# Filler matmuls, a re-sorted weight queue and a new operand order in the first stage of a hybrid SSD/Conformer layer

## The chip, the cores and the metric

The kernel runs on one core of a Trainium2 chip. The metric is the device time of one execution in microseconds (us), the median of three runs. A profiled execution gives the trace that the rows further down come from.

## What is computed

One layer of a hybrid backbone over 128 context tokens and 512 latent tokens, 1024 channels, in float32. The conditioning vector (one for the latent tokens, one for the context) is turned into six modulation vectors; the normed tokens are scaled and shifted by the first two of them and go through one input projection, which feeds an SSD mixer and a Conformer branch; an output projection and a gated ConvFFN follow. The change lies wholly in the first lines:

```python
def trunk_layer(x, cond, prm, init_f, init_b, rows):
    mod = jax.nn.silu(cond) @ prm["w_ada"] + prm["b_ada"]
    sh1, sc1, g1, sh2, sc2, g2 = [m[:, None, :] for m in jnp.split(mod, 6, axis=-1)]

    h = rms_norm(x, prm["norm_mix_pre"]) * (1 + sc1) + sh1
    proj = h @ prm["w_in"]
    z, xbc, dt_raw, cf_in = jnp.split(
        proj, [SSD_WIDTH, SSD_WIDTH + CONV_CH, SSD_WIDTH + CONV_CH + 2 * SSD_HEADS], axis=-1)
    ...
```

## The kernel before

The tokens lie with channels on the 128 partitions, as eight tiles T0 to T7 (channel block k) of 640 columns: 512 latent and 128 context tokens. "The first stage" is what runs until the first three products of the input projection are done, about the first 57 us.

**Norm.** ACT squares each token tile (L498), and TensorE adds up the squares over the channels with a column of ones (`colsum`, L473). That matmul is narrow: it writes 32 partitions, and four of them, one in each 32-column group of the array (`tile_position=(0, 32 * j)`), take a quarter of the tokens each. ACT takes the square root (L487), DVE the reciprocal (L488), and `spread` (L481) copies the result to all 128 partitions with four full-width matmuls. DVE multiplies the token tiles by it (L523).

**Condition.** `ada_first(s)` (L437 to L446) computes slice s of four: eight weight tiles of 128x512, 256 KB each, go against the condition `cts` in narrow matmuls again, four for each tile (L441). ACT copies the sum out (`adar`, L444), TensorE transposes it (L423), DVE adds the bias (`modv`, L432) and forms the factor `asc` (L529, L530). Slice s serves the channel blocks 2s and 2s+1: DVE applies it (L534) and splits the result into a high part on ACT (L400, tiles H0 to H7) and a low part on DVE (L402, H8 to H15).

**First products.** Three units of the input projection (g0, a0, B0) are accumulated in psum P0, P2 and P1. `mm3` (L415) makes every product of three full-width matmul pairs (384 and 256 columns): weight high x token low, high x high, low x high, where it is the first of a sum, and high x high first elsewhere. Unit weights arrive in `wr` (512 KB, L287), ACT takes their high part `wh` (L311) and POOL the low part `wl` (L313). `dt_product` (L507) is a narrow one again; L604 (`idhl`) is the last step of that branch.

**Queues and order.** Every transfer of the stage is issued by SP, one after the other: the condition, the eight token tiles, then the weight tiles of the four slices (slice 0 in T8 to T15, slice 1 in S4 to S11, slice 2 in M0 to M7 and HL, slice 3 in T8 to T15 again), the constants `csts`, the parameters `prms`, the weights of dt (`wdts`) and the units' `wr`. The order of the instructions on each engine is neither the program's nor a scheduler's: a table `ORDER` gives it by hand, one list of instruction numbers for each engine, and `issue_in_order` (L166) ties every instruction behind the one ahead of it in the list. In the table of before, the transfers of the slices are mixed with each other.

Of the kernel before, what the change touches and what calls it, by code (L numbers as in the profile page):

```python
# [13 lines left out]
P = 128  # L14
# [23 lines left out]
for _name, _w in (("b_ada", 48), ("g_mix_pre", 8), ("g_mix_post", 8), ("g_ffn_pre", 8),  # L38
# [12 lines left out]
0-31 36-49 32-34 50-53 35 54-90 104-105 102-103 91-101 116-119 106 120-126 107-115 127 187-191 175-180 192  # L51
181-182 193 173-174 140-172 194-196 183-186 211-242 197-198 258-259 243 128-129 246-252 260-263 130-139
199-210 270 253-257 264-265 284-289 244-245 282-283 320-327 271-281 290-291 266-269 296 292-294 308-311
297-298 295 312-319 299-307 328-332 341-374 399-402 375-378 403 379-385 404 386-388 405-434 447-450 435-445
451-464 446 465-487 495 488-492 496-506 493-494 507-522 543-550 523 551-560 524-535 561-567 536 568-574
537-542 575-590 645-648 333-335 649-684 336-339 685-690 693-719 691-692 720-725 340 389-393 726-758 789-796
759 394-398 797-799 760-768 595 591-594 800-803 769-776 804-818 777-788 819-836 878-916 596-603 608 604-607
926-931 917-923 932-946 924-925 947-970 974-983 971-973 984-1005 609-620 1006-1014 1022 621-644 1023-1028
1015-1019 1029 1020-1021 1030-1048 837-841 1070-1073 1049 1074-1087 1050-1056 1088-1094 1057-1069 1095-1117
846-849 842-845 854-857 850-853 1118-1146 1207-1213 1147 1214-1216 1148-1163 1217 1164-1165 874-877 858-873  # L60
1218-1226 1255-1256 1227-1249 1257-1275 1250-1251 1276-1283 1252-1254 1284-1290 1170 1166-1169 1291-1294
1303-1314 1295-1302 1315-1337 1351-1352 1338-1350 1353-1374 1450-1452 1375-1381 1453-1470 1382-1398
1171-1178 1183-1186 1179-1182 1471-1484 1187-1206 1485-1517 1546 1518 1547-1554 1519-1521 1399-1403
1522-1524 1555-1556 1525 1557-1567 1526-1532 1568-1577 1533-1545 1578-1609 1683-1684 1610-1623 1404-1408
1624-1626 1685-1700 1627-1641 1701-1718 1409-1432 1441-1442 1433-1435 1443-1444 1436-1440 1719-1723
1731-1743 1724-1729 1744-1745 1730 1746-1755 1449 1445-1448 1756-1811 1827-1830 1812-1814 1642-1646
1815-1823 1831-1835 1824-1826 1836-1866 1916 1867 1917-1918 1647-1682 1919 1868-1869 1920 1870-1874
1921-2010 2012-2017 2011 2018-2022 1875-1879 2023-2080 2149-2150 2081-2089 2151-2157 2090-2103 2158-2164
2104-2107 2165-2179 1884-1887 1880-1883 1892-1895 1888-1891 2197-2201 1912-1915 1896-1911 2202-2244
2180-2196 2357-2386 2112 2108-2111 2245-2272 2387-2416 2117-2120 2113-2116 2417-2446 2125-2128 2121-2124  # L70
2145-2148 2129-2144 2447-2467 2507-2518 2468 2519 2273-2276 2317-2320 2277-2280 2321-2324 2469-2476
2520-2531 2477-2491 2325-2335 2341-2344 2336-2340 2281-2290 2492-2495 2291-2300 2496-2506 2532 2301-2310
2533-2534 2311-2312 2345-2352 2535-2545 2313-2316 2546-2552 2567-2585 2553-2562 2586-2593 2563-2566 2594
2353-2356 2597-2613 2595-2596 2614-2615 2810-2829 2759-2770 2645-2648 2621-2637 2649 2638-2639 2650-2658
2640-2641 2659-2661 2642-2644 2693-2704 2616-2620 2669-2676 2705-2709 2662-2668 2717 2710-2711 2677-2682
2712 2683-2686 2718-2727 2687-2689 2728 2713 2729-2740 2714 2690-2692 2830-2831 2771-2780 2832-2835
2781-2790 2836-2841 2843 2741-2742 2715-2716 2792-2794 2743-2747 2791 2748-2755 2844-2847 2756-2758
2795-2799 2848-2849 2800-2809 2850-2860 2894-2896 2960-2963 2897-2915 2964-2966 2916-2924 2967-2973
2925-2926 2974-2987 2861-2892 2842 3092-3094 3026 2988-2990 3027-3035 2991-2992 3036-3045 3095 3046-3057
3096-3099 2893 3058 3125 3100-3102 2927-2942 2993-3014 2943-2950 3015-3024 2951-2958 3103-3107 2959  # L80
3108-3122 3126-3133 3123-3124 3134-3146 3203-3204 3147-3150 3025 3151-3158 3059-3089 3176-3183 3090
3159-3165 3205-3207 3166-3175 3184-3188 3208-3210 3189-3198 3211-3218 3199-3202 3091 3219-3236 3301-3310
3237-3245 3311 3246-3251 3312 3252-3253 3270-3276 3313-3317 3338 3318-3319 3277-3284 3320-3327 3332-3337
3339-3348 3254-3269 3285-3300 3328-3331 3349-3373 3388-3390 3397-3398 3380-3387 3374-3375 3399 3410-3412
3406-3409 3377 3376 3391-3393 3400-3402 3413-3415 3419 3422-3423 3378 3420 3379 3394-3396 3421 3403-3405
3424 3431 3416-3418 3425 3428 3426 3429 3432-3433 3430 3437-3439 3446-3448 3427 3434-3436 3471-3476 3443
3440-3442 3449-3451 3493-3504 3509-3510 3444-3445 3452 3511-3513 3539-3556 3455-3470 3477-3492 3514-3524
3505-3508 3557-3570 3525-3538 3453-3454 3572-3575 3644-3647 3668-3669 3576-3578 3648-3650 3670-3674
3579-3581 3571 3651-3653 3582-3584 3654-3656 3675-3680 3585-3587 3657-3659 3681-3682 3620-3623 3588-3590
3624-3625 3591-3593 3596-3598 3594-3595 3599-3619 3626-3643 3660-3667 3683-4059 4061-4081 4060 4082-5548  # L90
5597-5615 5549-5596 5616-5658 5693-5695 5659-5664 5696-5716 5665-5692 5717-6599 6665-6668 6600-6664
6669-6676""",
    "DVE": """
0 3-4 1-2 13-16 18-19 17 5 20 11-12 23-26 6 27-30 7-9 21-22 33-35 38-39 36 10 37 31-32 41-42 46 43-44 40 47
45 48 51 49 52 50 53-54 84-90 111-114 55-56 91-94 69 95-96 119-122 57-60 97-100 61-68 101-102 70-71 75
123-125 103-106 72 152-155 76-77 82 78 73 107-109 79-80 74 81 110 83 126-129 163 130-135 115-118 136 156
137-141 164-165 142-146 193 147-151 194-196 166-171 204 172-180 157-159 181 160 182-183 161 184 162 197
205-206 185-192 207-210 234 238-239 235-237 211 200 212 240-241 201 213-214 198-199 215-216 242-245 217-219
246 202-203 220-223 253 224-233 254-261 247 262-266 248-250 267 283-286 268 251-252 269 298 270-275 287
276-282 299-300 289 301-313 288 290-291 328-331 314 292-293 315 332 316-317 339 318 294 296 295 297 319-326  # L100
333 340-341 327 334 342-347 335 348 336 349 337-338 350-354 371-374 355-359 375 382 360-370 383-384 376
385-386 377 387-393 416-419 379 378 394-396 380 420 381 397-401 463 432 464-465 428 402-403 447 404 442
448-450 405-407 443 408-410 421-422 444 411 424 423 451 445-446 412-413 426 414-415 425 427 454 429-430 455
452-453 434 439 436 438 435 456 433 457 437 440 460 431 459 458 461-462 441 466-467 469-470 472 478 473
475-476 468 479-480 482-485 481 471 474 488 477 486 489 487 495 498 496 502 501 497 491 490 505 508 494
499-500 515 509 503-504 518 492 512 493 519 506-507 510-511 520-522 537 523 513-514 516 525 527-528 530 526
529 532-533 538 531 535 524 540 534 557 536 539 517 541-543 545 544 558 546 548 550 547 559 552 560-561
563-564 566 549 551 567 565 553 568 554-556 569 571-575 570 562 576-585 589 586-588 593 590 594 591-592 595
597 596 598 601-602 599-600 605 603-604 606-612 615-616 613-614 617-749 1053 750-1046 1049-1051 1047-1048
1052 1054-1063 1065 1064 1066-1075""",  # L110
    "Activation": """
0-3 7 6 4 8 5 9-11 15 18 12 19 17 21-22 13 20 24 23 25 35 26-27 32-33 14 30 28-29 16 48-49 47 31 56-58 61 64
50-51 62 34 67 65-66 63 52-53 37-38 79 116 80 54 36 39 55 71 68 40-43 120 44-45 72 46 117 121-122 81 69-70
59-60 73-76 82-83 123 91 96 77 86-90 110 92 101 97-98 133-134 99-100 112 108 166 78 84-85 124 135 106-107
102-104 170 127-128 125-126 167 93-94 105 95 111 171-172 114 113 109 115 129-130 173 183 156-157 131-132 141
146 136 151 137 152-155 142-143 174 158-159 186 177 144 178 184 187 165 164 138-140 175-176 160 145 161
147-150 118 162-163 179-180 190 189 222 119 188 185 191 197 192-193 181 194-196 216 223 207 226 208 198-200
229 182 227-228 214 201 230 212 202-203 213 233 204 217 231 234 232 215 239 209-210 205-206 218 211 219-221
235 168-169 236 274 240-241 275 237-238 278 244 254-255 245-248 242-243 249-250 259 268 260-262 256-258 270
263 271 279-282 291 285-286 283 264-265 284 266 251-253 269 324 287-288 272-273 267 224 292-293 325 328 289  # L120
# [1476 lines left out]
```

## Time and profile before

| | us |
|---|---|
| three runs | 983.82, 984.30, 982.83 |
| median | 983.82 |
| span of the profiled execution | 979.4 |
| median less that span (outside the span) | 4.4 |
| TensorE busy in the profiled execution | 944.5 |

The profiled span is divided into views. The page gives busy time by engine and by fortieths of the span. The windows give the same for stretches that one chooses, with the share of the 16 DMA engines that was busy. The timeline lists instructions in order of time, with the idle time ahead of a group in brackets and what ended it. TensorE has two timelines, one of its matmuls (PE) and one of its weight loads (PEld), which run ahead of the matmuls they belong to. Matmul records overlap by the depth of the array, so that the price of one is read from start to start, not from its length; a narrow matmul shows as 128*32, a full-width one as 128*128.

### The profile page before, as it was taken

The page shows a single profiled execution, that of the slowest core. Times are in us where ns is not written, and L with a number is a line of the kernel's source. Part 1 is how long each engine was busy: PE and PEld are TensorE (multiplying, and loading weights), DVE is VectorE, ACT ScalarE, POOL GpSimd, SP SyncE. Part 2 cuts the span into 40 slices and gives each one's busy share as a digit, 9 for nine tenths or more (in the row PEclk, how much of TensorE's full clock was granted, in tenths as well). Part 3 has the DMA queues.
Part 4 walks back from the last instruction along what each step waited for, and adds up shares of the span by engine and source line. Part 5 has one row for each costly group of instructions (what it writes and reads, how often), then busy time and mean ns, then how long its engine had stood idle before and what let it go on. Part 6 is the DMA issues. An engine that isn't in the chain of part 4 may idle for free.

```text
span 979.4 us, 18795 instructions
## 1 busy us (share of the span) xinstructions
PE 944.5 (96%) x7623; PEld 920.9 (94%) x7623; DVE 686.9 (70%) x1076; ACT 471.3 (48%) x799; POOL 577.9 (59%) x416
## 2 busy tenths in 40 slices
PE   4999999999999999999999999999999999999995
PEld 3799999999999998998889999999999999999995
DVE  1769898999989997523585998998988898400004
ACT  4355666877668477622464852323232336322211
POOL 1334699889999882534662994444454436543434
PEclk9999999999999999999999999999999999999998
DMA  9622424433424422578662322222222231322213
GB/s 347 250 72 86 117 82 127 146 95 123 139 80 142 128 91 93 196 244 303 200 218 88 129 86 69 84 78 73 86 66 86 66 87 54 94 69 76 82 38 108
DMA packets 50294, 117.52 MB, mean 120 GB/s; under 512 B 6016, under 2 KB 13952, under 8 KB 50208
## 3 DMA queue, kind: packets, MB, share of 16 engines
q1 hardware_dynamic: 50208, 116.33, 37.2%
q8 instruction: 60, 0.98, 0.4%
q14 instruction: 26, 0.21, 0.1%
HBM read 112.55 MB, written 3.75 MB: 119 GB/s over the span
## 4 chain that ended last, share of the span: by engine, by line
PE 87%; DMA 3%; ACT 3%; DVE 2%; SPq 1%; POOL 1%; issue 1%; POOLq 0%; ACTq 0%; DVEq 0%
PE ps L415 72%; PE ps L1259 3%; PE pq L415 2%; PE pq L818 2%; PE pq L807 1%; PE pq L460 1%; SPq L452 1%; DMA wr<-in_wout 1%; PE pq L744 1%; PE pq L441 1%; POOL wl L313 1%; PE pq L473 1%; DMA S<-acD 1%; ACT wh L311 1%; DMA T<-in_wada 1%
## 5 line engine op out<-in xcount | busy, mean ns | idle before, releaser
L313 POOL TENSOR_TENSOR wl<-wr,wh 128x1024 fp32r<-128x1024 f32 (+3 forms) x127 | 290.4, 2290 | 316.3 <-ACT wh L311 299.2
L415 PE MATMUL ps<-H,wh 128*128 128x384 f32 (+1 forms) x1636 | 315.7, 309 | 0.1
L311 ACT ACTIVATE wh<-wr 128x1024 fp32r<-128x1024 f32 (+3 forms) x131 | 131.3, 1003 | 316.2 <-PE ps L415 183.2
L415 PE MATMUL ps<-T,wh 128*128 128x384 f32 (+1 forms) x1472 | 272.5, 306 | 1.8 <-ACT S L1227 1.8
L1237 DVE SCALAR_TENSOR_TENSOR S<-ps,prms,S 128x441 f32<-128x441 f32 (+2 forms) x336 | 233.5, 695 | 29.4 <-ACT S L1227 18.9
L415 PEld LDWEIGHTS ps<-H,wh 128*128 128x128 f32 x1636 | 249.0, 188 | 2.7 <-issue 1.7
L415 PEld LDWEIGHTS ps<-T,wh 128*128 128x128 f32 x1472 | 218.9, 188 | 2.2 <-ACT S L1227 2.1
L872 DVE SCALAR_TENSOR_TENSOR ps<-u,prms,ps 128x655 f32<-128x655 f32 x205 | 185.1, 903 | 10.8 <-ACT ps L869 4.8
L415 PE MATMUL ps<-H,wl 128*128 128x384 f32 (+1 forms) x818 | 191.8, 309 | 0.0
L415 PE MATMUL ps<-T,wl 128*128 128x384 f32 (+1 forms) x736 | 166.2, 305 | 0.0
L415 PEld LDWEIGHTS ps<-H,wl 128*128 128x128 f32 x818 | 129.0, 188 | 1.0 <-issue 1.0
L415 PEld LDWEIGHTS ps<-T,wl 128*128 128x128 f32 x736 | 113.0, 188 | 0.0
L488 DVE RECIPROCAL rsm<-rsm 128x160 f32<-128x160 f32 (+2 forms) x9 | 7.4, 817 | 147.1 <-ACT rsm L487 147.1
L415 PE MATMUL ps<-S,wh 128*128 128x384 f32 (+1 forms) x420 | 88.0, 310 | 1.6 <-ACT wh L311 1.6
L415 PEld LDWEIGHTS ps<-S,wh 128*128 128x128 f32 x420 | 66.5, 188 | 2.8 <-ACT wh L311 1.8
L415 PE MATMUL ps<-S,wl 128*128 128x384 f32 (+1 forms) x210 | 54.9, 309 | 0.3 <-POOL wl L313 0.3
L789 ACT ACTIVATE S<-S,AC 128x128 f32<-128x128 f32 x140 | 45.5, 392 | 2.4 <-DMA S<-acD 2.4
L885 POOL TENSOR_TENSOR T<-T,T 128x640 f32<-128x640 f32 x20 | 32.0, 1602 | 12.5 <-ACT T L881 12.5
L1227 ACT ACTIVATE S<-ps,prms 128x640 f32<-128x640 f32 x42 | 36.5, 869 | 0.0
L415 PEld LDWEIGHTS ps<-S,wl 128*128 128x128 f32 x210 | 35.2, 188 | 0.9 <-POOL wl L313 0.5
L881 ACT ACTIVATE T<-u,prms 128x512 f32<-128x512 f32 (+1 forms) x54 | 27.9, 554 | 6.8 <-POOL T L885 6.8
L1339 POOL TENSOR_TENSOR H<-S,S 128x640 f32<-128x640 f32 x16 | 25.3, 1581 | 0.0
(346 smaller groups left out, 1180.3 us busy)
## 6 DMA issues: line engine op xcount, KB each, us to landing
wr<-in_wup SPq DMA_DIRECT2D x44, 512.0 KB, 3.5
wr<-in_win SPq DMA_DIRECT2D x36, 512.0 KB, 3.9
T<-in_wada SPq DMA_DIRECT2D x49, 256.0 KB, 5.4
S<-acD SPq DMA_DIRECT2D x28, 320.0 KB, 4.7
wr<-in_wdown SPq DMA_DIRECT2D x16, 512.0 KB, 3.4
wr<-in_wout SPq DMA_DIRECT2D x13, 512.0 KB, 4.5
H<-in_wada SPq DMA_DIRECT2D x23, 256.0 KB, 4.6
S<-in_wada SPq DMA_DIRECT2D x16, 256.0 KB, 5.4
```

The lines of the kernel that those rows point to most:

```text
L311: ac.activation(hi[:, :n], raw[:, :n], AF.Copy)
L313: lo_eng.tensor_tensor(lo[:, :n], raw[:, :n], hi[:, :n].bitcast(F32), SUB)
L415: last_mm[0] = te.matmul(out, w, x[:, c0:c1], start=first and i == 0, stop=last and i == 2)
L789: ac.activation(rc, rc, AF.Relu, scale=-1.0, bias=AC2[:, c, row:row + 1])
L818: te.matmul(py[64 * h:64 * h + 64, i * P:(i + 1) * P], xt[:, c * P + 64 * h:c * P + 64 * h + 64], rs[h, d][:, c * P:(c + 1) * P], start=d ...
L872: ve.scalar_tensor_tensor(acc, u[:, j:j + UO], w(j), acc, MUL, ADD)
L881: ac.activation(t[:, b:c], u[:, a:a + c - b], AF.Copy, scale=w(j))
L885: gp.tensor_tensor(far, far, t, ADD)
L1227: ac.activation(out, v, AF.Identity, bias=prm_col("ffn_b", i), scale=w(1, 1))
L1237: ve.scalar_tensor_tensor(ob, vl[:, r0 + a - 1:r1 + a - 1, q0 + b - 1:q1 + b - 1], w(a, b), ob, MUL, ADD)
L1259: te.matmul(pt[:, o:o + c1 - c0], w[k] if i in (1, 2) else w[:, k * P:(k + 1) * P], x[:, c0:c1], start=k == 0 and j == 0, stop=k == KD - 1 ...
L1339: gp.tensor_tensor(f_raw[q], a, b, MUL)
```

## The change

In words: 48 "filler" matmuls are added (`keep_busy`). Each multiplies ones with ones, 128x128 in float32 and full width, into columns 896 to 1024 of psum P0, which the product of unit g0 does not use. They read nothing but the constant `ones`. In the three first products the first of the three matmul pairs takes the tokens' high part (`lo_first=False`). The table `ORDER` is written anew for the first stage on every engine; behind it the lists are the same, renumbered by 48 on TensorE.

```diff
-    def mm3(pt, hi, lo, j, xh, xl, first, last, halves=(0, 1), places=None):
+    def mm3(pt, hi, lo, j, xh, xl, first, last, halves=(0, 1), places=None, lo_first=True):
...
-        for i, (w, x) in enumerate(((w1, xl), (w1, xh), (w2, xh)) if first else ((w1, xh), (w1, xl), (w2, xh))):
+        for i, (w, x) in enumerate(((w1, xl), (w1, xh), (w2, xh)) if first and lo_first else ((w1, xh), (w1, xl), (w2, xh))):
...
     firsts = [(get_unit(unit_of[n][0]), psum((0, 2)[i])) for i, n in enumerate(FIRST[:2])]
+    every = ones.to_broadcast([P, P])
+
+    def keep_busy(out, n):
+        for _ in range(n):
+            te.matmul(out, every, every, start=True, stop=True)
+
+    keep_busy(firsts[0][1][:, 896:1024], 48)
...
-                mm3(pt, whi, wlo, k, h_hi[k], h_lo[k], k == 0, k == KD - 1)
+                mm3(pt, whi, wlo, k, h_hi[k], h_lo[k], k == 0, k == KD - 1, lo_first=False)
```

The new lines move the numbers of all later ones by 7; L517 is the filler. Of the table one line stands here, the first of TensorE's list before and SP's list before and after:

```diff
-0-31 36-49 32-34 50-53 35 54-90 104-105 102-103 91-101 116-119 106 120-126 107-115 127 187-191 175-180 192
...
-0-8 14 24 10 13 16 11 9 12 15 23 19 17 31 27 25 18 20 26 28-29 41 47 30 36 34-35 38 40 21 43 39 37 44-45 42
+0-13 19 14-18 20 24-28 21 29-31 34-41 23 42-49 32-33 22 50 52-57 72 81 51 59-61 82 58 64 62 83 63 87 96 68
```

TensorE at the start, before: the sums of squares (L473), then slice 0 of the condition (L441 on T8 to T15) with the spread (L481) in between. A row is a line, the tile written, the tiles read, the shape, and how many follow each other.

```order
L473 MATMUL pq1_17_127<-S0_22_152,ones_107 32x160 x4
L473 MATMUL pq1_17_127<-S1_23_158,ones_107 32x160 x4
L473 MATMUL pq1_17_127<-S2_24_164,ones_107 32x160 x4
L473 MATMUL pq1_17_127<-S3_25_170,ones_107 32x160 x4
L441 MATMUL pq0_55_265<-T8_9_89,cts_69 32x128 x4
L441 MATMUL pq0_55_265<-T9_10_91,cts_69 32x128 x4
L441 MATMUL pq0_55_265<-T10_11_93,cts_69 32x128 x4
L441 MATMUL pq0_55_265<-T11_12_95,cts_69 32x128 x2
L481 MATMUL ps1_26_176<-rsm_27_177,csts_87 128x160 x3
```

TensorE in the same place, after, from the sum of squares of x5 on (11 fillers stand ahead of the first of these sums, one ahead of x3's, five between x3's and x5's).

```order
L473 MATMUL pq1_17_127<-S1_23_158,ones_107 32x160 x4
L517 MATMUL ps0_29_204<-ones_107 128x128 x3
L473 MATMUL pq1_17_127<-S2_24_164,ones_107 32x160 x4
L517 MATMUL ps0_29_204<-ones_107 128x128 x2
L473 MATMUL pq1_17_127<-S3_25_170,ones_107 32x160 x4
L517 MATMUL ps0_29_204<-ones_107 128x128
L441 MATMUL pq0_55_313<-T8_9_89,cts_69 32x128 x4
L517 MATMUL ps0_29_204<-ones_107 128x128 x2
L441 MATMUL pq0_55_313<-T9_10_91,cts_69 32x128 x4
L517 MATMUL ps0_29_204<-ones_107 128x128 x2
L441 MATMUL pq0_55_313<-T10_11_93,cts_69 32x128 x4
L517 MATMUL ps0_29_204<-ones_107 128x128 x2
```

Between two narrow groups there now stand one to three full-width fillers.

TensorE at slice 1 of the condition (tiles S4 to S11), before: the narrow matmuls follow each other, with two products and two dt matmuls in between.

```order
L441 MATMUL pq0_58_318<-S4_31_214,cts_69 32x128 x4
L441 MATMUL pq0_58_318<-S5_32_216,cts_69 32x128 x4
L441 MATMUL pq0_58_318<-S6_33_218,cts_69 32x128 x4
L441 MATMUL pq0_58_318<-S7_34_220,cts_69 32x128 x4
L441 MATMUL pq0_58_318<-S8_35_222,cts_69 32x128 x4
L441 MATMUL pq0_58_318<-S9_36_224,cts_69 32x128 x2
L415 MATMUL ps0_29_204<-H8_61_362,wh0_188 128x384
L415 MATMUL ps0_29_204<-H8_61_362,wh0_188 128x256
```

The same place after; wh0 and wh1 are the high parts of units g0 and a0, H0 the tokens' high part of block 0, H8 its low part.

```order
L441 MATMUL pq0_58_366<-S5_32_264,cts_69 32x128 x4
L517 MATMUL ps0_29_204<-ones_107 128x128
L441 MATMUL pq0_58_366<-S6_33_266,cts_69 32x128 x4
L415 MATMUL ps0_29_204<-H0_60_408,wh0_188 128x384
L415 MATMUL ps0_29_204<-H0_60_408,wh0_188 128x256
L415 MATMUL ps2_30_211<-H0_60_408,wh1_194 128x384
L441 MATMUL pq0_58_366<-S7_34_268,cts_69 32x128 x4
L415 MATMUL ps2_30_211<-H0_60_408,wh1_194 128x256
L441 MATMUL pq0_58_366<-S8_35_270,cts_69 32x128 x4
L415 MATMUL ps0_29_204<-H8_61_410,wh0_188 128x384
```

The products of slice 0 start ahead of the end of slice 1's sums and are cut by them tile by tile.

SP's queue behind the token tiles, before (T12, T8, T11 are slice 0's, S4 slice 1's):

```order
L246 DMA T12_13_97<-in_wada1 128x512
L246 DMA S4_31_214<-in_wada1 128x512
L246 DMA T8_9_89<-in_wada1 128x512
L246 DMA T11_12_95<-in_wada1 128x512
L246 DMA T14_15_101<-in_wada1 128x512
L246 DMA T9_10_91<-in_wada1 128x512
L237 DMA csts_87<-in_cst 128x384
```

and after, from the same point on:

```order
L237 DMA csts_87<-in_cst 128x384
L246 DMA T8_9_89<-in_wada1 128x512
L246 DMA T9_10_91<-in_wada1 128x512
L246 DMA T10_11_93<-in_wada1 128x512
L246 DMA T11_12_95<-in_wada1 128x512
L287 DMA wr0_186<-in_win 128x1024
L246 DMA T12_13_97<-in_wada1 128x512
```

The tiles of a slice now come in the order of their use, slice by slice, with wr0, wr1 and wr2 among slices 0 and 1; the 32 tiles and wr0, wr1, wr2 still stand ahead of wr3, and the rest of the parameters has moved ahead of wr3 too.

## Rows read from the trace of the kernel before

**Rows 1.** The page, busy time by engine and TensorE in 40 slices.
```profile
PE 944.5 (96%) x7623; PEld 920.9 (94%) x7623; DVE 686.9 (70%) x1076; ACT 471.3 (48%) x799; POOL 577.9 (59%) x416
...
PE   4999999999999999999999999999999999999995
```
**Rows 2.** Windows: stretch, length, busy time (records) by engine, PEclk, DMA share, GB/s.
```profile
5.40:13.80 8.40, 2.06 (x24) 0.64 (x24) 0.00 (x0) 3.90 (x6) 0.00 (x0) 1.00 1.02 377
...
22.20:28.50 6.30, 4.59 (x72) 2.06 (x73) 5.97 (x12) 2.59 (x4) 2.38 (x1) 1.00 1.06 390
...
38.70:57.60 18.90, 18.90 (x198) 17.69 (x198) 8.41 (x19) 8.55 (x14) 5.21 (x5) 1.00 0.12 44
57.60:120.00 62.40, 62.40 (x437) 61.98 (x437) 57.49 (x97) 36.07 (x66) 32.08 (x17) 1.00 0.35 108
120.00:180.00 60.00, 58.58 (x441) 57.92 (x440) 54.36 (x74) 42.28 (x89) 54.45 (x51) 1.00 0.38 107
```
**Rows 3.** Waits of TensorE, 0 to 62 us: total, times, longest.
```profile
PE pq L473 <- ACT S L498: 11.7, 3, 5.5
```
**Rows 4.** Timeline of TensorE's matmuls: start, length, group, count, idle before.
```profile
13.80 2.90 PE L473 MATMUL pq<-S,ones 128*32 128x160 f32 x40 [1.53 <-ACT S L498]
16.47 1.92 PE L441 MATMUL pq<-T,cts 128*32 128x128 f32 x28
...
19.98 0.43 PE L441 MATMUL pq<-T,cts 128*32 128x128 f32 x8
20.33 0.54 PE L481 MATMUL ps<-rsm,csts 128*128 128x160 f32 x2
20.80 1.07 PE L441 MATMUL pq<-T,cts 128*32 128x128 f32 x28
```
**Rows 5.** Timeline of TensorE's weight loads, where the matmul form changes.
```profile
19.97 0.16 PEld L441 LDWEIGHTS pq<-T,cts 128*32 128x32 f32 x8 [0.17 <-issue]
20.33 0.30 PEld L481 LDWEIGHTS ps<-rsm,csts 128*128 128x128 f32 x2 [0.20 <-issue]
20.80 0.80 PEld L441 LDWEIGHTS pq<-T,cts 128*32 128x32 f32 x28 [0.17 <-issue]
...
38.73 1.69 PEld L441 LDWEIGHTS pq<-T,cts 128*32 128x32 f32 x64 [0.18 <-issue]
40.61 0.30 PEld L415 LDWEIGHTS ps<-H,wl 128*128 128x128 f32 x2 [0.20 <-issue]
...
50.02 0.42 PEld L415 LDWEIGHTS ps<-H,wh 128*128 128x128 f32 x3 [0.20 <-issue]
```
**Rows 6.** Token tiles' transfers (line L234): count, issue times; time to landing.
```profile
L234 SPq DMA_DIRECT2D T<-in_xT x8: 421/432/476, 1.2 to 4.5; - x8
...
DMA to landing us min/median/max: 3.0/5.4/6.5
```
**Rows 7.** Timeline of ACT: one square, one copy of a slice's sum.
```profile
14.68 0.74 ACT L498 ACTIVATE S<-T 128x640 f32<-128x640 f32 x1 [0.93 <-ACT S L498]
...
21.91 0.28 ACT L444 ACTIVATE adar<-pq 128x128 f32<-128x128 f32 x1 [2.24 <-PE pq L441]
```
**Rows 8.** The chain that ended last: start, length, what (a full-width 128x128 float32 matmul).
```profile
130.05 0.67 PE pq L744 x6
```
**Rows 9.** Timeline of TensorE's matmuls, later in the stage.
```profile
38.73 1.96 PE L441 MATMUL pq<-T,cts 128*32 128x128 f32 x64
...
43.91 0.73 PE L415 MATMUL ps<-H,wh 128*128 128x384 f32 x4
44.48 0.45 PE L415 MATMUL ps<-H,wl 128*128 128x384 f32 x2
...
48.59 1.50 PE L507 MATMUL pq<-T,wdts 128*32 128x512 f32 x24
...
56.58 1.20 PE L604 MATMUL pq<-idhl,T 128*128 128x32 f32 x10
57.61 0.83 PE L415 MATMUL ps<-H,wh 128*128 128x384 f32 x4
```

## What I predicted, and from what

> **What bounds the kernel now.** I read the page first: TensorE is busy 944.5 of 979.4 us, and all its forty slices but the first and the last are full [rows 1]. Behind the first stage there is little to win or lose: from 57.6 to 120 us TensorE works in 62.40 of 62.40 us, from 120 to 180 in 58.58 of 60 [rows 2]. So the stage hands its end on: each microsecond by which the first product of the next unit (57.61 us, [rows 9]) moves is one of the whole. I count that it arrives undiminished.
>
> Then the stage itself, in windows. Up to 28.5 us the DMA engines are full (shares 1.02 and 1.06, 377 and 390 GB/s) and TensorE is not: 2.06 of 8.40 us, then 4.59 of 6.30; from 38.7 on the DMA share is 0.12 and TensorE has 18.90 of 18.90 [rows 2]. In the first part the transfers set the pace, in the last TensorE alone does. The longest wait is that of the sums of squares (L473) for ACT, 11.7 us in three pieces [rows 3]: the tile order in that queue, nothing lost later as long as the weights are late as well.
>
> The clock: the forty narrow records from 13.80 us (five groups of eight) take 2.67 us, 0.53 a group; the 28 of L441 from 20.80 cost 0.22 for a group of eight, which is the higher level [rows 4]. So TensorE ran at 1.2 GHz through its stretch from 13.80 and at 2.4 GHz by 20 us; it had waited before that. I take twice the higher level's price for the lower.
>
> **The change part by part.** The fillers fill the waits of TensorE, so in the changed kernel I ask where TensorE stops waiting, and what it has to do from there to the end of the stage.
>
> Start: the token tiles land between 4.2 us (1.2 + 3.0) and 11.0 us (4.5 + 6.5) [rows 6]. A tile is 320 KB, 0.84 us at 390 GB/s, so x3, the fourth, lands four tiles before the last, at 7.7 us; its square takes 0.74 [rows 7], and the sum of x3 can start at 8.6. What is ahead (11 fillers, three sums, one filler) fits: 12 x 0.45 + 3 x 0.53 = 7.0 us at the low clock, if TensorE begins by 1.6 us. It also holds TensorE at work from the start, so I take the high clock from x3 on.
>
> Work of TensorE from 8.6 us to L604, at the high clock:
> - Five sums of squares, half of 0.53: 1.3.
> - 36 fillers. The chain has six records of a 128x128 float32 matmul in 0.67 us, two records each, so 0.223 [rows 8]: 8.0.
> - 32 weight tiles of the condition: 64 records are eight tiles, from 38.73 to 40.41 (the next load at 40.61 less its 0.20 of waiting) [rows 5, 9], 0.21; with the 0.22 of [rows 4]: 7.0.
> - Four passes of the spread at 0.27 (160 columns against 128 of the filler's 0.223): 1.1. Four transposes at half a filler: 0.4.
> - 72 pairs of first products: four records, two pairs, from 43.91 to 44.48 [rows 9], 0.287 each: 20.7.
> - The dt matmuls: 48.59 to 50.02 is 1.4 [rows 9] for half of them; all: 3.2.
>
> Sum 41.7. The same prices give 18.9 for the unbroken stretch from 38.73 to 57.61, the trace's length, so the list is complete but for one thing.
>
> **The change of form.** Where the matmuls go from narrow to full width or back, TensorE's weight loads stand idle for 0.17 to 0.20 us, for nothing that the profile shows [rows 5]. It costs the matmuls too: from 19.98 to 20.80 there are one group of eight and one pass of the spread, 0.22 + 0.27 = 0.49 us of work in 0.82 us [rows 4], so 0.33 for two changes, 0.165 each. The mean of the six idle times is 0.19; I take 0.18, between. Before, the stage has 15 such changes, mostly beside waits for weights. After, each group of fillers between two narrow groups makes two, and so do the products cut by slice 1's tiles: counted in the order, 54 to L604, 51 of them behind x3. That is 51 x 0.18 = 9.2 us.
>
> The Trainium skill says the same of the cause: TensorEngine Tiling (Array Packing), section Key Properties, states that changing the tiling mode drains the TensorE. It gives no price; by that rule this kernel pays at each of the 54 changes, and the trace agrees with its 0.17 to 0.20.
>
> So L604 comes at 8.6 + 41.7 + 9.2 = 59.5 us against 56.58: +2.9. With the ends of that price: 51 x 0.165 = 8.4 gives +2.1, 51 x 0.19 = 9.7 gives +3.4.
>
> Does TensorE really not wait? A slice-0 tile with its two fillers and two changes takes 0.22 + 0.45 + 0.36 = 1.03 us; a 256 KB tile lands every 0.67 (390 GB/s). So it falls behind the queue; T8 is begun at 8.6 + 1.3 + 11 x 0.223 + 10 x 0.18 = 14.2, when all tokens, csts and T8 to T10 (three times 0.67 behind 11.5) are there. The sum of slice 0 ends at about 23 us (before: 21.91, [rows 7]), slice 1's follows at about 32, and the last weight, landed by 38.7 in either order since the same bytes stand ahead of it, is wanted only at about 44. What was the bound before, the queue, is then covered throughout; its new order gains nothing. If that cover is gone the case is the first rival.
>
> Edits with one answer: the squares in order of landing end with x7 as before, at 11.8; the reload of ACT's table before the square root stands in ACT's idle time (0.93 and more ahead of a square, [rows 7]), as do wh1 and wh2 earlier. DVE's multiplications of x2 and x3 go ahead of modv, beside TensorE's fillers. High part first frees the first products from the low part on DVE, under 1 us a slice, beside which TensorE now has other work: nothing. Three times 18 pairs, 5.2 us each, cover the chain of copy, transpose, modv and split between the slices.
>
> **The rivals.** (A) The changes of form cost nothing where the next work is ready, or the order of loads hides them: then TensorE needs 41.7 us plus one or two for late tiles of slice 1, and L604 comes at 51.5 to 54. For it: most of the changes in the trace stand beside other waits, and 48.59 to 50.02 has several idle stretches of its own. Against: [rows 4] shows the matmuls late with both loads and data ready. Gain 2.6 to 5, about 980.3. (B) Half the price, 0.09 a change: L604 at about 55 to 57, 983.6, no change. (C) The clock rises late, since the narrow groups and short waits don't hold it up: the lower level until 13 to 19.6 us costs half of the time spent so far, 2.2 to 5.5 us more: 989 to 992. It decides when the rise comes behind about 10 us. For it: before, the clock rose only in a stretch without waits [rows 4]; against: eleven fillers in a row start the kernel now.
> The skill's TensorE: Matmul & The Clock Gate, Part 1, says that the default is the throttled clock and activity releases it; by that rule the fillers bring the rise forward, which the sum already has, and no run here shows it yet.
>
> **How the numbers follow.** The profiled span is 979.4, 4.4 under the median of 983.82; I add the shift to the median: 983.8 + 2.9 = 986.7. The forecast's own range is 985.6 to 988.0, by the ends of the price and a clock that rises a microsecond or two late. Chances: forecast 0.60, A 0.13, B 0.16, C 0.11. The range over all, 982.3 to 989.6, holds the forecast, B and the lower part of C, and leaves out A and the rest of C. What a measurement of this kernel can tell from no change is about 0.2%, 2.0 us; A and a bit of B are faster by that (0.13), the rest of B and the lowest of the forecast (under 985.8) are within it (0.23), the rest is slower (0.64).
>
> **What would show it.** In the profile of the changed kernel: full-width records of L517 at about 0.11 a record between narrow ones with 0.17 to 0.20 of idle loads at every change (right), or loads without idle time (A). TensorE busy with no wait for DMA after 9 us; the sum of slice 0 copied (adar) at about 23 us and slice 3's at 46 to 47; L604 at 59 to 60. Sums of squares at 0.27 a group from x3 on, or at 0.53 (C). If L604 comes at or ahead of 56.6 the forecast is wrong; if it comes at 59.5 and the whole is not later, the handing on is.

## The result, and the profile after

The changed kernel takes 986.5 us (median of 22 runs, 983.06 to 989.99) against 982.69 for the kernel before on the same chips; the ratio is 1.0044, with a 95% interval of 1.0033 to 1.0054, so it is 4.3 us slower. I had forecast 986.7 from a median of 983.82, 2.9 us slower. The profiled span is 984.5 us against 979.4. It lies 2.0 us under its run's time, and other executions of the kernel before lie as much under theirs; the profiled one of before lies 4.4 under the median, so it is a quick one, and a difference of two spans may be off by 2 us. The end of the first stage, read within one execution, is surer.

The windows of the changed kernel answer to [rows 2] (stretch, length, busy time and records by engine, PEclk, DMA share, GB/s):

```profile
5.40:13.80 8.40, 6.62 (x86) 3.92 (x78) 0.00 (x0) 6.18 (x8) 0.00 (x0) 1.00 1.03 376
13.80:22.20 8.40, 8.40 (x98) 6.09 (x95) 3.71 (x5) 1.45 (x2) 2.35 (x1) 1.00 1.05 393
22.20:28.50 6.30, 4.90 (x58) 3.55 (x57) 4.83 (x10) 2.17 (x4) 2.34 (x1) 1.00 1.03 389
28.50:38.70 10.20, 10.20 (x128) 7.82 (x128) 7.92 (x16) 3.18 (x5) 2.40 (x1) 1.00 1.06 392
38.70:60.50 21.80, 21.80 (x217) 18.62 (x217) 8.10 (x23) 8.69 (x15) 4.01 (x6) 1.00 0.10 37
```

From 5.4 to 13.8 us TensorE worked 2.06 us before and works 6.62 now; from 13.8 on it is full but for one hole between 22.2 and 28.5. The transfers run as before. The timeline of its matmuls (start, length, group, count, idle time before and its releaser), which answers to [rows 4, 9]:

```profile
0.87 4.24 PE L517 MATMUL ps<-ones 128*128 128x128 f32 x22 [0.87 <-POOL epsc L257]
...
13.82 0.49 PE L517 MATMUL ps<-ones 128*128 128x128 f32 x2
14.24 0.43 PE L441 MATMUL pq<-T,cts 128*32 128x128 f32 x8
14.59 0.71 PE L517 MATMUL ps<-ones 128*128 128x128 f32 x4
15.23 0.43 PE L441 MATMUL pq<-T,cts 128*32 128x128 f32 x8
...
26.52 0.42 PE L441 MATMUL pq<-S,cts 128*32 128x128 f32 x8
28.34 0.73 PE L415 MATMUL ps<-H,wh 128*128 128x384 f32 x3 [1.40 <-ACT H L400]
...
60.99 1.20 PE L611 MATMUL pq<-idhl,T 128*128 128x32 f32 x10
62.02 0.83 PE L415 MATMUL ps<-H,wh 128*128 128x384 f32 x4
```

Its weight loads, which answer to [rows 5]:

```profile
14.59 0.52 PEld L517 LDWEIGHTS ps<-ones 128*128 128x128 f32 x4 [0.20 <-issue]
15.23 0.16 PEld L441 LDWEIGHTS pq<-T,cts 128*32 128x32 f32 x8
15.59 0.52 PEld L517 LDWEIGHTS ps<-ones 128*128 128x128 f32 x4 [0.20 <-issue]
```

One weight tile with its two fillers takes 15.23 - 14.24 = 0.99 us. The work in it is 0.22 + 2 x 0.223 = 0.67; two changes of form would make up the rest, 0.16 each (narrow_fill below tests it). The loads wait 0.20 us at each change to full width. L611 (L604 before) starts at 60.99 against 56.58 [rows 9], 4.41 us later, and the first product of the next unit as much.

The sum of slice 0 is done where the prediction had it (adar at 23.02). Then comes the hole. It begins with DVE; the timeline of all engines from 24.3 us in the changed kernel:

```profile
24.32 2.34 POOL L313 TENSOR_TENSOR wl<-wr,wh 128x1024 fp32r<-128x1024 f32 x1 [4.31 <-ACT wh L311]
24.37 2.31 DVE L537 TENSOR_TENSOR asc<-asc,prms 128x4 f32<-128x4 f32 x1
```

L537 works on four columns and takes 0.16 us elsewhere. Here it lasts 2.31, to 26.68, just behind the end of POOL's split at 26.66. What follows on DVE (L541) and ACT (H0) is late by that, and TensorE, out of fillers, waits 1.40 us.

### The profile page after: what moved, and what is told of

The parts are those of the page before. It is cut to its first block, busy times and chain, and to the rows that moved or that the text cites. A ratio compares the mean times of both kernels' runs of the same rounds, so it can differ in the third digit from the quotient of the medians.

```text
span 984.5 us, 18997 instructions
## 1 busy us (share of the span) xinstructions
PE 958.8 (97%) x7719; PEld 931.9 (95%) x7719; DVE 687.3 (70%) x1076; ACT 474.5 (48%) x801; POOL 576.6 (59%) x416
## 4 chain that ended last, share of the span: by engine, by line
PE 89%; ACT 3%; DMA 3%; DVE 2%; POOL 2%; issue 1%; SPq 0%; POOLq 0%; ACTq 0%; DVEq 0%
PE ps L415 73%; PE ps L1266 3%; PE pq L415 2%; PE pq L825 2%; PE pq L814 1%; PE pq L460 1%; DMA wr<-in_wout 1%; POOL wl L313 1%; PE ps L517 1%; PE pq L441 1%; PE pq L751 1%; DMA S<-acD 1%; PE pq L473 1%; ACT wh L311 1%; DMA T<-in_xT 1%
## 5 line engine op out<-in xcount | busy, mean ns | idle before, releaser
L1244 DVE SCALAR_TENSOR_TENSOR S<-ps,prms,S 128x441 f32<-128x441 f32 (+2 forms) x336 | 233.5, 695 | 29.4 <-ACT S L1234 18.9
```

The source lines that it names most:

```text
L1244: ve.scalar_tensor_tensor(ob, vl[:, r0 + a - 1:r1 + a - 1, q0 + b - 1:q1 + b - 1], w(a, b), ob, MUL, ADD)
```

## The experiments

Ten kernels, each profiled once and timed 4 to 10 times beside the kernel before. The kernel before had a median of 982.70 us beside the first four, 983.27 beside the next four and 981.66 beside the last two, so the ratios compare across the rows and the medians do not. "Changes" are changes of form up to L611, counted in the order; "slice 0" is the start of the first adar copy. L611 has other line numbers in some kernels, since a few lines came or went above it.

| kernel | changes | slice 0, us | L611, us | median, us | ratio to before (95%) |
|---|---|---|---|---|---|
| before | 15 | 21.91 | 56.58 | | |
| changed | 54 | 23.02 | 60.99 | 986.50 | 1.0044 (1.0033 to 1.0054) |
| narrow_fill | 25 | 21.16 | 60.31 | 983.34 | 1.0005 (0.9987 to 1.0023) |
| none_fill | 25 | 19.21 | 58.16 | 982.17 | 0.9996 (0.9982 to 1.0010) |
| front_fill | 26 | 20.04 | 58.78 | 984.21 | 1.0010 (0.9993 to 1.0026) |
| half_fill | 54 | 32.67 | 73.81 | 994.85 | 1.0120 (1.0083 to 1.0156) |
| wh1_early | 54 | 22.92 | 59.40 | 984.67 | 1.0017 (1.0005 to 1.0028) |
| group_early | 46 | 24.92 | 60.12 | 983.55 | 1.0000 (0.9987 to 1.0013) |
| low_first | 54 | 24.86 | 63.71 | 990.27 | 1.0086 (1.0062 to 1.0111) |
| mid_group | 21 | 19.37 | 55.36 | 977.41 | 0.9957 (0.9938 to 0.9975) |
| none_group | 17 | 18.75 | 57.73 | 981.89 | 1.0000 (0.9982 to 1.0018) |
| mid_group2 | 19 | 18.73 | 55.14 | 977.95 | 0.9958 (0.9945 to 0.9971) |

**What a change of form costs: narrow_fill.**

```diff
         for _ in range(n):
-            te.matmul(out, every, every, start=True, stop=True)
+            for j in range(4):
+                te.matmul(out[32 * j:32 * j + 32, :], ones.to_broadcast([P, 32]), every, start=True, stop=True,
+                          tile_position=(0, 32 * j))
```

> Every filler of the changed kernel is split into four narrow matmuls, one in each 32-column group, in the same place: the same work for TensorE (the four run side by side), but between narrow neighbours no change of form is left, 25 changes to the last step of the stage (L611) where the changed kernel has 54. Theory (a change of form costs TensorE 0.165 to 0.19 us, and TensorE is the bound from 9 us on): 29 changes less are 5 us less work; the sum of slice 0 (adar) comes at 19.5 instead of 23.0, the wait for H0 grows to about 2.3, and L611 starts at about 57.3 instead of 60.99, so the whole is 3.5 us under the changed kernel and 0.7 over the kernel before. Rival (changes of form are free, the fillers' own work and the new order cost the time): L611 stays at 61, the whole at 4.3 over the kernel before.

Its timeline of TensorE's matmuls:

```profile
13.13 0.40 PE L444 MATMUL pq<-T,cts 128*32 128x128 f32 x8
13.34 0.62 PE L521 MATMUL ps<-ones 128*32 128x128 f32 x16
13.79 0.40 PE L444 MATMUL pq<-T,cts 128*32 128x128 f32 x8
...
17.20 0.27 PE L521 MATMUL ps<-ones 128*32 128x128 f32 x1 [1.04 <-issue]
...
26.20 0.73 PE L418 MATMUL ps<-H,wh 128*128 128x384 f32 x3 [1.36 <-ACT H L403]
...
28.59 0.74 PE L418 MATMUL ps<-H,wl 128*128 128x384 f32 x2
29.12 1.27 PE L418 MATMUL ps<-H,wh 128*128 128x384 f32 x4
30.19 0.52 PE L418 MATMUL ps<-H,wl 128*128 128x384 f32 x1
```

and its windows, TensorE's alone (stretch, length, busy time and records, PEclk, DMA share, GB/s):

```profile
28.00:30.00 2.00, 2.00 (x8) 0.50 1.05 391
```

The same tile with the same two fillers now takes 13.79 - 13.13 = 0.66 us: the work alone. In the changed kernel it was 0.99. Nothing but the form of the fillers differs, so two changes cost 0.33 us, 0.165 each: the price of the prediction, shown. The rival that they are free falls. The gain to L611 came out smaller than I expected, though, 0.7 us for 3.7, and the rows say why. Slice 0 is ready 1.9 us earlier and not 3.5, since TensorE now waits elsewhere: 1.04 us just ahead of the spread (the row at 17.20), and 2.4 us for squares where the changed kernel waits 1.8. The first products start 2.1 us earlier, but from 27.9 to 31 us they run at half speed (four records, two pairs, from 29.12 to 30.19 instead of 0.57). The granted clock from 28 to 30 us is 0.50, the 1.2 GHz level. TensorE had been busy for 3.91 of the 4 us from 20 to 24 us, and still the clock fell, behind the wait of 1.36 us for H0; the changed kernel waits 1.40 us there and keeps its clock.

That wait has its cause on DVE, which is late beside a split on POOL, as in the changed kernel but at another operation: the four of L546 (L541 in the changed kernel, 1.52 us there) take 3.44.

```profile
22.45 2.38 POOL L316 TENSOR_TENSOR wl<-wr,wh 128x1024 fp32r<-128x1024 f32 x1 [2.79 <-ACT wh L314]
...
22.65 3.44 DVE L546 TENSOR_SCALAR T<-T,asc,modv 128x512 f32<-128x512 f32 x4
```

The whole gained 3.9 us of span over the changed kernel, more than L611. TensorE's waits behind the stage account for most of it: from 170 to 200 us the changed kernel waits 1.0 us and this one not at all, from 400 to 490 us 5.5 against 3.6.

**What the fillers are good for: none_fill and front_fill.** The call is left out, or has 11 in place of 48; the table loses the numbers.

```diff
-    keep_busy(firsts[0][1][:, 896:1024], 48)
+    keep_busy(firsts[0][1][:, 896:1024], 11)
```

> The 48 fillers are taken out, all else is the changed kernel: 25 changes of form. Theory: the sum of slice 0 at about 18.8 (the weights' landing sets it), TensorE waits at every tile until 23 us, L611 at 55.7, the whole 0.9 us under the kernel before, if the clock is high by the first products at 23. Rival (the fillers are there for the clock, and without them it stays low): the first products run at 0.57 a pair instead of 0.287 for some 4 to 6 us, L611 at 58 to 59, the whole 1.5 to 2.5 over the kernel before.

> Only the 11 fillers ahead of the first sum of squares stay, the other 37 are taken out: 26 changes of form. Theory: as without fillers (sum of slice 0 at 18.8, L611 at 55.7, whole 0.9 under the kernel before), and the sums of squares at 0.27 a group. Rival (the clock falls again while TensorE waits from 9 to 23 us): groups of L441 at 0.43 instead of 0.22, first products at 0.57 a pair, L611 at 58 to 59.

TensorE's windows of none_fill:

```profile
20.00:24.00 4.00, 2.42 (x27) 0.72 1.05 403
24.00:28.00 4.00, 4.00 (x26) 0.50 1.05 389
28.00:32.00 4.00, 4.00 (x40) 0.92 1.06 384
```

and of front_fill:

```profile
8.00:12.00 4.00, 3.02 (x40) 0.68 1.04 402
12.00:16.00 4.00, 3.90 (x47) 0.50 1.05 404
24.00:30.00 6.00, 6.00 (x39) 0.51 1.06 389
```

Both tell the same. Without fillers slice 0 is ready at 19.21, 2.7 us ahead of the kernel before: that is the worth of the new table, of the queue, the order of the squares and the earlier rise of the clock together (eight passes of the spread take 1.35 us at 15.29 us here, six take 1.64 at 18.40 before); the runs do not part them. TensorE then waits (2.42 of 4.00 us busy from 20 to 24), the clock falls to 0.50, and the first products pay for it from about 23 to 28.4 us. L611 comes at 58.16, as the rival had it (58 to 59); the whole is even with the kernel before, between the two. The fillers at the very start alone are no help: their high clock is gone by 12 us, comes back between 16 and 24 (0.97 and 0.89) and is gone again for the first products. So fillers are not useless: they hold the clock. In the changed kernel the clock of every such window is 1.00, and its products run at 0.287 to 0.30 a pair.

**Shorter fillers: half_fill.**

```diff
-            te.matmul(out, every, every, start=True, stop=True)
+            te.matmul(out[:, 0:64], every, every[:, 0:64], start=True, stop=True)
```

> Every filler writes 64 columns instead of 128, so it costs TensorE 0.11 instead of 0.223; places and the 54 changes of form stay. Theory: 36 x 0.11 = 3.9 us less work from 9 us on, of which the wait for H0 gives back about 0.5: L611 at 57.6, the whole 3.4 under the changed kernel. Rival (the fillers only fill waits): L611 at 60 to 61 as in the changed kernel.

Its timeline of TensorE's matmuls:

```profile
9.42 1.54 PE L519 MATMUL ps<-ones 128*128 128x64 f32 x6
10.89 0.76 PE L475 MATMUL pq<-S,ones 128*32 128x160 f32 x8
11.59 1.12 PE L519 MATMUL ps<-ones 128*128 128x64 f32 x4
...
39.25 1.22 PE L417 MATMUL ps<-H,wh 128*128 128x384 f32 x3
...
44.41 0.43 PE L443 MATMUL pq<-S,cts 128*32 128x128 f32 x8
```

Less filler made the kernel 12 us slower than the kernel before in the median (the profiled execution, 998.49 us, is the longest of four; the shortest took 990.72), so theory and rival both missed. A sum of squares takes 0.70 us from start to start with one change (10.89 to 11.59), where the changed kernel, at the high clock, takes 0.41; the first products still run at half speed at 39.25, and the price of the higher level comes back between 43 and 44.4 us, behind a stretch of real products. TensorE was at work without a break from 8.7 us on. A filler of 64 columns still loads a full 128x128 weight, and it costs 0.43 us here (three with one change 1.47, two 1.04), hardly less than the 0.45 I took for one of 128 columns at the low clock: the shorter fillers saved next to nothing and the clock stayed down. (The column PEclk reads 1.00 in these windows, as it does for the first 19 us of the kernel before [rows 2], whose rows stand at the lower level too [rows 4]: ahead of the first change of an execution only the rows tell.) Why it stayed down, and why it fell with narrow fillers, the runs do not settle.

**The missing 1.4 us: wh1_early.** The head of ACT's list, two numbers exchanged (11 is wh0, 12 wh1, 15 the first adar copy):

```diff
-1 0 2-11 15 12 18-19 13 17
+1 0 2-12 15 18-19 13 17
```

> The changed kernel with one exchange in ACT's list: wh1 (the high part of unit a0) stands ahead of the copy of slice 0's sum instead of behind it, so POOL splits off wl1 (L313) from about 21.8 to 24.2 us instead of 24.32 to 26.66. In the changed kernel a small DVE operation of slice 0 (L537) took 2.31 us instead of 0.16, to the end of that POOL operation, and TensorE then waited 1.40 us for H0. Theory (DVE's operation was held by POOL's): L537 back at 0.16, no wait for H0, L611 at 59.4 instead of 60.99, the whole 1.5 us less. Rival (the long L537 has a cause of its own, or TensorE is late anyway): L537 stays over 2 us, or L611 at 60.7 to 61.

DVE's timeline:

```profile
24.06 0.17 DVE L538 TENSOR_SCALAR asc<-modv 128x4 f32<-128x4 f32 x1
24.27 0.16 DVE L539 TENSOR_TENSOR asc<-asc,prms 128x4 f32<-128x4 f32 x1
```

and the waits of TensorE, 0 to 62 us (total, times, longest):

```profile
PE pq L475 <- ACT S L500: 1.2, 4, 0.3
PE ps L519 <- POOL epsc L259: 0.9, 1, 0.9
```

POOL's split now runs from 21.74 for 2.35 us. The small operation is back at 0.16 us, the wait for H0 is gone, L611 stands at 59.40 as expected, and the ratio to the kernel before falls from 1.0044 to 1.0017, 2.7 us where I expected 1.5 (the intervals are about 1 us wide to either side). DVE had been held by POOL. Not every DVE operation is: the four of L532, which read psum, take 0.75 us each from 27.55 on, beside POOL's next split (27.77 to 30.16), as much as elsewhere. The Trainium skill's SBUF — State Buffer, section SBUF: two separate sides, says that DVE and GpSimd (POOL in the rows) share a port pair, that a DVE operation with two SBUF inputs needs it when the GpSimd operation reads SBUF too, and that the one that starts first keeps it for its whole instruction. The trace agrees: in the changed kernel POOL started at 24.32, L537 at 24.37, and L537 ended with POOL.

The same row stood in the trace of before, off the path that mattered there; I had it and did not read it (timeline of all engines from 25.8 us):

```profile
25.81 2.38 POOL L313 TENSOR_TENSOR wl<-wr,wh 128x1024 fp32r<-128x1024 f32 x1 [3.68 <-ACT wh L311]
...
26.39 2.48 DVE L402 TENSOR_TENSOR H<-T,H 128x640 fp32r<-128x640 f32 x1
```

**The cut products: group_early.** Part of TensorE's list, slice 1 (129 to 148 are S7 to S11, 152 to 175 products); M7, HL and the dt matmuls likewise:

```diff
-152-153 164 129-132 165 133-136 154-162 137-140 163 166-167 141-144 168-170 145-148 171-174 149
+152-153 164-165 129-136 154-163 166-170 137-148 171-174 149
```

> As the kernel with wh1 early, and the products of slices 0 and 1 are no longer cut by single tiles of the condition: S7 and S8 together, S9 to S11 together, M7 and HL together with the dt matmuls. 46 changes of form instead of 54, all 48 fillers stay. Theory: 8 x 0.168 = 1.3 us less than with wh1 early alone, L611 at 58.1. Rival (the cuts stood in waits for weights and cost nothing): L611 as with wh1 early alone or later.

L611 is at 60.12, later than with wh1 early alone. But slice 0 was 2.00 us late (24.92 against 22.92), and up to there the two kernels are the same. In this execution the sum of x3 came 0.73 us later, after a wait of 1.42 us for its square (9.18 against 8.45), and then the clock was down, which cost the rest (TensorE's window, as above):

```profile
8.00:12.00 4.00, 2.83 (x22) 0.65 1.03 386
```

From slice 0's sum to L611 it is 35.20 us here and 36.48 with wh1 early: 1.28 us less for eight changes, 0.16 each, as expected. The medians, 983.55 against 984.67, go the same way, though their intervals overlap.

**The order of operands: low_first.**

```diff
-                mm3(pt, whi, wlo, k, h_hi[k], h_lo[k], k == 0, k == KD - 1, lo_first=False)
+                mm3(pt, whi, wlo, k, h_hi[k], h_lo[k], k == 0, k == KD - 1)
```

> The changed kernel with the old order of operands in the first products (tokens' low part first at k = 0), all else as changed. Theory: the first product now waits for H8, DVE's low part, instead of H0, ACT's high part: 0.8 us more at the wait that is 1.40 us in the changed kernel, L611 at 61.8, the whole 0.8 over the changed kernel. Rival (the operand order is covered by other work of TensorE, as the prediction had it): L611 at 61.0.

The first product in the timeline of TensorE's matmuls:

```profile
31.05 0.73 PE L417 MATMUL ps<-H,wh 128*128 128x384 f32 x3 [2.26 <-DVE H L404]
```

TensorE waits 2.26 us for H8 instead of 1.40 for H0: 0.86, as expected. The rest of L611's 2.7 us came ahead of slice 0, which was 1.84 us late: again a later sum of x3 (0.34 us) and a clock that fell early (0.70 from 8 to 12 us). From slice 0 to L611 it is 38.85 against 37.97 us, 0.88 more. So high part first is worth 0.9 us in this kernel; my "nothing" was wrong as long as TensorE waits there. The whole is 4.1 us over the changed kernel by the ratios, not 0.8. Its four runs have a lower mean granted clock (0.989 to 0.993, the changed kernel's 0.992 to 0.996); whether the longer wait brings that about was not tried.

**Putting it together: mid_group, none_group, mid_group2.** mid_group keeps ten fillers (three ahead of the transpose of slice 0, four behind it, three between S4 and S6), has the products uncut, and wh1 behind H0 and H1 on ACT (the head of its list). none_group has no fillers. mid_group2 also moves S7 and S8 ahead of the first products.

```diff
-    keep_busy(firsts[0][1][:, 896:1024], 48)
+    keep_busy(firsts[0][1][:, 896:1024], 10)
...
-1 0 2-11 15 12 18-19 13 17
+1 0 2-11 15 18-19 12-13 17
```

> Ten fillers only, the ones around the transpose of slice 0 and between S4, S5 and S6; products not cut by single tiles (as in the kernel before this one in the list); wh1 behind H0 and H1 on ACT. 21 changes of form. Theory: slice 0's sum at 19 us as without fillers, first products at about 23; if the ten fillers hold the clock high from there, L611 at 54.6 and the whole 2 us under the kernel before; if the clock is low from 23 to 28 us as it was without fillers and with the front ones alone (products at 0.57 a pair), L611 at 56.5 to 57.5 and the whole about even.

> The kernel with ten fillers around slice 0's transpose and uncut products (55.36 us to L611, 0.43% under the kernel before), less its ten fillers: 17 changes of form. Theory (those fillers hold the clock through TensorE's waits between 19 and 24 us): without them the granted clock falls to the lower level at about 23 to 28 us, as in the other kernel without fillers, and L611 comes at 56.5 to 57.5, the whole 1 to 2 us over the kernel with ten. Rival (the ten fillers only cost their own changes of form; the uncut products made the gain): L611 at 54.8 to 55.4, the whole as with ten fillers or 0.5 less.

> The same kernel with its ten fillers, and S7 and S8 also moved ahead of the first products, so that slice 1 is cut once (19 changes of form instead of 21). Theory: 2 x 0.168 = 0.3 us less, L611 at 55.0, the whole 0.3 less. Rival (S8 lands at 23.9 us, and products that could have started wait for it): L611 at 55.4 or later.

TensorE's windows of mid_group:

```profile
20.00:24.00 4.00, 3.27 (x41) 1.00 1.05 396
24.00:28.00 4.00, 4.00 (x47) 1.00 1.05 389
```

and of none_group:

```profile
20.00:24.00 4.00, 1.72 (x25) 0.88 1.05 402
24.00:28.00 4.00, 4.00 (x27) 0.50 1.06 390
```

Ten full-width fillers in TensorE's waits ahead of the first products keep the granted clock at 1.00, without them it is 0.50 from 24 to 28 us. The timed runs say the same: their mean granted clock is 0.994 to 0.996 with the ten and 0.990 to 0.994 without. L611: 55.36 against 57.73; the whole, by the ratios, 4.2 us less. The rival, that the uncut products alone made the gain, falls. mid_group was 0.8 us later than I hoped (54.6), and is still faster than the kernel before by 0.43% (interval 0.25% to 0.62%) and, by the two ratios, than the changed one by 8.5 us, to which fewer fillers, uncut products and a DVE that POOL does not hold all contribute.

Only 1.22 of the 4.2 us under the kernel before stand at L611. The rest comes behind the stage. A spread (L481) much later, in the kernel before:

```profile
477.52 1.03 PE L481 MATMUL pq<-rsm,csts 128*128 128x96 f32 x8
```

and in mid_group, with TensorE's window behind it:

```profile
473.64 1.03 PE L481 MATMUL pq<-rsm,csts 128*128 128x96 f32 x8
...
480.00:484.00 4.00, 3.50 (x16) 0.58 0.34 104
```

It is 3.88 us earlier. On the way TensorE waits less: not at all from 170 to 200 us (0.7 before), and 0.5 us for weight tiles between 450 and 460 us (2.0 before). Why a lead of 1.2 us shortens those waits is not shown. In this execution the clock then falls once, 0.58 from 480 to 484 us, and gives half of the lead back.

mid_group2 is 0.22 us better at L611 (0.3 expected) and the same in the whole; the intervals do not part the two.

## Why the prediction was right, and where its sum was short

- **TensorE becomes the bound.** Held. T8 begins at 14.24 (I had 14.2), slice 0 ends at 23.02 (23), and no wait for a transfer stands behind x3. The new table's gain, 2.7 us at slice 0 where no filler stands in the way (none_fill), was eaten by fillers and changes, as the sum said.
- **The change of form.** Held, and shown by narrow_fill: 0.165 each. I took 0.18, so 51 of them were 0.8 us too dear.
- **The fillers' work.** 0.223 each held in the rows at the high clock.
- **What the sum missed.** L611 came 4.41 us later, not 2.9. The step that failed is "three times 18 pairs cover the chain of copy, transpose, modv and split": the first slice has no products ahead of it, only fillers, and its chain was 2.15 us longer than its rows because POOL held DVE. TensorE waited 1.40 us; wh1_early removes that and gives 59.40, against the predicted 59.5; the sums of slices 1 and 3 (34.13 and 48.66, for 32 and 46 to 47) were late for the same reason. For the same reason "high part first: nothing" was wrong: it was worth 0.9.
- **The handing on.** 4.41 us at L611, 4.3 in the whole by the ratio (3.2 to 5.3). It held for the changed kernel within that interval, while narrow_fill and mid_group showed that waits between 170 and 490 us can add some 3 us to what the stage gains.
- **Rival A and B** are out, by 0.99 against 0.66 us. **Rival C** did not come in the changed kernel, which is where the fillers do their work: its rows are at the high level by 5.1 us, earlier than my 8.6. But its mechanism is real: the clock fell in the kernels with narrow fillers, with none and with the front ones alone, and in two of the profiled executions with all 48 at full width (group_early, low_first), between 8 and 16 us.

The sum is also right in part by luck. The 59.40 of wh1_early meets my 59.5 because two errors cancel: the changes were 0.8 us too dear, and the first products about 0.7 too cheap. From 50.19 to 55.57 the changed kernel runs eighteen pairs at 0.299 each, where I took 0.287; at that price the sixty pairs ahead of 57.4 us would be 0.7 us more. From 58.41 on a pair takes 0.287; why it took more ahead of that is not shown.

```profile
50.19 0.45 PE L415 MATMUL ps<-H,wl 128*128 128x384 f32 x2
...
55.57 0.46 PE L415 MATMUL ps<-H,wl 128*128 128x384 f32 x2
```

My check of the list should have warned me: its prices, with the 1.03 us of L604, give 18.3 us for the stretch from 38.73 to 57.61, not the 18.9 that I wrote. That the total came out at 986.5 for 986.7 is luck, too: the shift was 4.3 us and not 2.9, and the kernel before took 982.69 and not the 983.82 that I added to. The lower end of my range, 985.6, is 0.3 under what my cheapest price gives.

## What to carry to other kernels

Work that is put into a wait costs its own time once the wait is gone, and it also costs where it is of another form than its neighbours: 0.165 us for each change between narrow and full-width matmuls here, so that 48 fillers of 0.22 us brought 29 changes with them. Put a few fillers into the waits just ahead of the work that needs the clock, in few groups, and let the products behind run uncut: ten of full width and 128 columns, in four groups, did what 48 did for the clock, and the kernel got faster. One block of them was not tried. Then count what you gain in the whole and not at the end of the stage alone: the two differed by 3 us here. Look in the trace for operations that last many times their usual length beside another engine's, even off the path: a new order can put them on it.

## What I had not expected of the hardware

- TensorE busy without a break from 8.7 to 43 us, with full-width fillers of 64 columns, stayed at the lower clock (12 us lost in the median); with fillers of 128 columns it was at the higher one by 5.1 us. Narrow fillers of the same length brought the higher clock as early, but after a wait of 1.36 us it fell to 0.50, while the changed kernel kept it through one of 1.40.
- Two executions with the same instructions up to slice 0 (wh1_early, group_early) differ by 2.00 us at its end, 0.73 by a later square and the rest by a fall of the clock between 8 and 16 us. The spread between runs of the changed kernel (983.06 to 989.99 us) goes with the clock in part: the nine with a mean granted clock of 0.993 have a median of 988.2, the four with 0.996 one of 985.2.
- A DVE operation on four columns took 2.31 us beside a POOL operation of 2.34, and 0.16 away from it; four on 512 and 128 columns took 3.44 beside one of 2.38, and 1.52 away from it.
